# Pinning the background operations of a two-layer encoder kernel in traced order

## The chip, the cores and the metric

The kernel runs on one core of a Trainium2 chip. The metric is the device time of one execution in microseconds (us): the median of three runs of the kernel before is 1942.75 us (1942.09 to 1945.22).

## The reference

Two layers work on x of 256 rows by 2048 channels, in float32. Each layer norms its input, makes one wide projection, runs two branches on parts of it, gates and adds them, and projects once more:

```python
def hybrid_layer(x, cos, sin, norm_g, w_in, ...):
    h = rmsnorm(x, norm_g)
    proj = h @ w_in
    (c_a, c_glu, c_gate, q_down, kv_down, k_pe, m_gate, g_conv, g_mla) = jnp.split(proj, idx, axis=-1)
    y_conv = conv_branch(c_a, c_glu, c_gate, conv_w, conv_b, conv_ln_g, conv_ln_b) @ w_proj_conv
    y_mla = mla_branch(q_down, kv_down, k_pe, m_gate, cos, sin, ...) @ w_proj_mla
    y = jax.nn.sigmoid(g_conv) * y_conv + jax.nn.sigmoid(g_mla) * y_mla
    return x + y @ w_out
```

The convolution branch is a gated linear unit, a causal depthwise convolution of width 31, a layer norm over the channels, SiLU, and a SiLU gate (`c_gate`). The attention branch brings queries, keys and values up from two low-rank parts (16 heads; 128 channels without and 64 with rotary position), norms queries and keys per head, attends with a mask in chunks of 64 rows, and multiplies by a SiLU gate (`m_gate`).

## The kernel before

**Products.** Every matrix product has the activations as stationary operand and streams the weights. To keep float32 accuracy with a faster matmul format, each weight value is split into a high part and a low remainder: `split` (L178) casts a slice of the weights on ScalarE (ACT, L187) and subtracts on VectorE (DVE, L188). A slice is 128 x 1024 values (two blocks of 128 rows, up to 512 columns). For each slice TensorE (PE) issues 12 matmuls: high by high, low by high, high by low (L240 to L242), for two halves of the rows and two blocks. There are 344 slices per layer, 688 in all; `split_p` has three buffers for the high parts and three for the low ones. Weights come from HBM in pieces of two slices, through SyncE's (SP) DMA queue, into three buffers (`load`, L166).

**The order of a layer** is a list of products (`order_of_layer`, L88). Slices, counted within a layer: three blocks of the low-rank parts ("down", slices 0 to 23), two of the gated linear unit ("glu", 24 to 39), then eight times a head pair's queries and keys with values ("uq" and "ukv", two slices each) with a block of eight slices behind them: glu 2 to 7 behind the first six pairs, and the first block of the convolution's gate ("cgate" 0) behind the seventh. The eighth pair has none behind it and ends at slice 127. In before there follow mgate, gmla, pmla (32 slices each, 128 to 223), cgate 1 to 3 (224 to 247), gconv (248 to 279), pconv (280 to 311) and wout (312 to 343).

**Evacuation.** `product` (L228) traces its matmuls and then an evacuation of the two results from PSUM, which has four buffers for results (`acc`). `uq_evac` (L495) copies queries and sums their squares on ACT (L498 to L502); `ukv_evac` (L508) does so for keys and values; `glu_evac` (L682), `cgate_evac` (L838) and `mgate_evac` (L804) apply sigmoid or SiLU. `wout_evac` (L870) loads a block of the residual through SP (L873), adds it (L874), and stores it: to the output in the last layer (L876).

**Background.** After each slice `product` calls `background` (L205): one slot. It runs what is due at this slot and then, by a budget, entries of the list `fill`: 31 taps per block of the convolution (L707 on DVE, the first on ACT, L704), then the layer norm (`mean`, `centre`, `var`, `apply`: L726 to L756) and the gate's multiplication (`gated`, L845 to L859). The budget's slots are set when the first mgate product begins: 19 x 8 - 4 slots are to use up the list, and what is left is traced at the first pconv product (`drain`). For each head pair `attention` (L523) sets due slots:

```python
            def stats_soon():
                with tc.high_priority(offset=60):
                    stats()
            at_slot(STATS_AT, stats_soon)
            at_slot(QK_OUT_AT, lambda: out("qk", rows))
            at_slot(QK_BACK_AT, lambda: back_in("qk"))
```

`stats` (L527 to L553) turns the sums of squares into factors (a reciprocal root by a shift and three iterations, L293 to L298), scales the keys and rotates the queries. Then the rows are written to HBM and read back, turned in blocks of 32 (`park` L253, `fetch` L264, on GpSimd's (POOL) DMA queue); DVE transposes inside the blocks (L572), ACT and DVE split them into high and low parts (L578 to L592), PE makes the scores (L600 to L616), DVE masks them and takes maxima (L605 to L624), ACT takes exponentials with their sums (L630), DVE their reciprocal (L636). The probabilities go the same way round (L642, split by L645 and L646), and PE multiplies them by the values (L655, copied out by L659).

**What sets the order.** Each engine works through its own list in order. The kernel is traced in the order above; a scheduler then builds each engine's list by priority (traced earlier is more urgent), from its own estimate of when operands are ready. `tc.high_priority(offset=n)` makes operations as urgent as if they had been traced n instructions earlier; the slice splits have 100. `tc.keep_in_program_order` (a pin) ties one instruction behind the instruction that was traced just before it on the same engine, whatever that is. `tc.issue_after` ties a block behind a given slice's low part. In before the taps and the DMAs of `park` and `fetch` are pinned; statistics, splits, masks, norms, gates and the residual loads are not.

Of the kernel before, what the change touches and what calls it, by code (L numbers as in the profile page):

```python
# [87 lines left out]
def order_of_layer():  # L88
# [25 lines left out]
def trunk(ctx: ExitStack, tc: tile.TileContext, xT, x, g_in, pos, win, wuq, wukv, wpc, wpm, wo, cst, rows, invf, out):  # L114
    nc = tc.nc
    pool = lambda name, bufs, **kw: ctx.enter_context(tc.tile_pool(name=name, bufs=bufs, **kw))
# [136 lines left out]
    def park(src, n, home):  # L253
        d = home.tile([4, 32, 4, n // 4], F32, tag=f"t{n}", name="turn_d")
        for i in range(4):
            tc.keep_in_program_order(
                nc.gpsimd.dma_start(  # L257
                    d[:, :, i, :].rearrange("j s e -> s j e"),
                    src[32 * i : 32 * i + 32, :].rearrange("s (j e) -> s j e", j=4),
                )  # L260
            )
        return d

    def fetch(d, z):  # L264
        tc.keep_in_program_order(nc.gpsimd.dma_start(z, d.rearrange("j s i e -> (j s) (i e)")))
# [6 lines left out]
    def turn(src, n, use, dst=None):  # L272
# [14 lines left out]
    def rsqrt(y, ms):  # L287
# [5 lines left out]
        nc.vector.tensor_scalar(ti, ms.bitcast(I32), 1, None, op0=ALU.logical_shift_right)  # L293
        nc.vector.tensor_scalar(yi, ti, -1.0, RSQRT_SEED, op0=ALU.mult, op1=ALU.add)
        for _ in range(3):
            nc.vector.tensor_mul(t, y, y)
            nc.vector.scalar_tensor_tensor(t, t, -0.5, ms, op0=ALU.mult, op1=ALU.mult)
            nc.vector.scalar_tensor_tensor(y, t, 1.5, y, op0=ALU.add, op1=ALU.mult)  # L298

    def rms_factor(out_ap, sums, n):  # L300
        ms = small.tile(list(sums.shape), F32, tag=f"ms{sums.shape[-1]}", name="ms")
        nc.vector.tensor_scalar(ms, sums, 1.0 / n, EPS, op0=ALU.mult, op1=ALU.add)
# [94 lines left out]
    for l in range(DEPTH):  # L397
# [125 lines left out]
        def attention(b, pair_of=pair_of, ss_d=ss_d, kpe=kpe, ccq=ccq, ssq_t=ssq_t, gqk=gqk, nope_t=nope_t, rope_t=rope_t, rope_k=rope_k, rope_l=rope_l, o_sb=o_sb, pt_h=pt_h, pt_l=pt_l, rinv=rinv):  # L523
# [3 lines left out]
            def stats():  # L527
                ss, qk = p["ss"], p["qk"]
                nc.vector.tensor_add(ss[:, 1], ss[:, 1], ss_d[:, 2, :].unsqueeze(2).broadcast_to([P, T, 2]))
# [4 lines left out]
                nc.vector.tensor_scalar(rs, r[:, 0], float(QK**-0.5), None, op0=ALU.mult)  # L534
                st["rs"] = rs
                for t in range(T):
                    rk = r[:, 1, t, :]
                    k = qk[:, t, :, 2:4, :]
                    nc.vector.tensor_mul(k, k, rk.unsqueeze(1).unsqueeze(3).broadcast_to([P, 4, 2, 32]))
                    nc.vector.tensor_mul(  # L540
# [8 lines left out]
                nc.vector.tensor_mul(qa.rearrange("p t a h c -> p (t a) h c"), qr, both(ccq))  # L549
                nc.vector.tensor_mul(qb.rearrange("p t a h c -> p (t a) h c"), qr, both(ssq_t))  # L550
                out = qk[:, :, :, 4, :].rearrange("p t (h a) c -> p t h a c", h=2)
                nc.vector.tensor_sub(out[:, :, :, 0, :], qa[:, :, 0], qb[:, :, 1])
                nc.vector.tensor_add(out[:, :, :, 1, :], qb[:, :, 0], qa[:, :, 1])  # L553
# [14 lines left out]
            def blockwise():  # L568
                for t in range(T):
                    z = p["qk"][:, t].rearrange("p j i c -> p (j i c)")  # L570
                    with tc.issue_after(newest[0]):
                        nc.vector.transpose(z, z)  # L572

            def split_nope(which):
                z = back[:, :, 2 * which : 2 * which + 2, :].rearrange("p b h s -> p h b s")
                hi, lo = (nope_t[:, 2 * which + i].rearrange("p h (b s) -> p h b s", s=32) for i in range(2))
                if which == 0:
                    nc.scalar.activation(z, z, AF.Copy, scale=gqk)  # L578
                nc.scalar.copy(hi, z)
                nc.vector.tensor_sub(lo, z, hi.bitcast(F32))  # L580

            def split_rope(which):
                z = back[:, :, 4 + which, :]
                rt, rl = (a.rearrange("p i h (b s) -> p i h b s", s=32) for a in (rope_t, rope_l.unsqueeze(1)))
                for h in range(2):
                    own, other = halves[h], halves[1 - h]
                    nc.scalar.copy(rt[own, which, h], z[own])
                    if which == 0:
                        nc.vector.tensor_sub(rt[other, 0, h], z[own], rt[own, 0, h].bitcast(F32))
                    else:  # L590
                        nc.scalar.copy(rt[other, 1, h], z[own])
                        nc.vector.tensor_sub(rl[own, 0, h], z[own], rt[own, 1, h].bitcast(F32))  # L592

            def scores():
# [9 lines left out]
                nc.scalar.copy(sx, s0[:, :, 1, :])  # L604
                nc.vector.tensor_add(sx, s0[:, :, 0, :], sx)  # L605
# [443 lines left out]
```

## Time and profile before

| | |
|---|---|
| median of three runs | 1942.75 us (1942.09 to 1945.22) |
| profiled execution | 1944.88 us; its span from first to last instruction 1943.1 us |
| mean granted TensorE clock | 0.995 |
| PE, DVE, ACT, POOL busy | 98%, 83%, 57%, 19% of the span |
| slice splits, ACT L187 and DVE L188 | 688 each, 704.5 and 813.8 us |
| convolution taps, DVE L707 | 960, 412.7 us |
| residual loads of layer 2, SP L873 | 8 of 256 KB, 6.2 us to landing (median) |

A line of a group names source line, engine, operation, the tiles written and read with their shapes, and the count; then busy time in us, mean ns of one, the idle time of the engine just before them and what ended most of it. A line of a stretch gives, for its 40 us, the busy time and the instructions of PE, PE's weight loads, DVE, ACT and POOL, the granted clock, the share of DMA time and GB/s. A line of the timeline begins with its start and length in us; a bracket at its end names idle time before it and what ended it. Matmuls are pipelined, so their lengths overlap; their distance from start to start tells the pace.

### The profile page before, as it was taken

Reading aid. Unit: us, or ns where it says so; the run is one execution under the profiler, and the core shown is the slowest. Engines: PE = TensorE matmul, PEld = TensorE weight load, DVE = VectorE, ACT = ScalarE, POOL = GpSimd, SP = SyncE. Lnnn points to the kernel's source line nnn. Section 1 sums busy time; section 2 is a strip of 40 time slices with the busy share of each in tenths; the row PEclk is TensorE's granted clock in tenths of the full one; section 3 lists DMA queues with packets and bytes.
Section 4 is the critical chain, followed back from the end, with each engine's and each line's share of the span. In section 5 each row is a group of like instructions: output and inputs, shape, how many; then the busy total and the mean of one; then the engine's idle time right before and its main releaser. Section 6 shows DMA issues by size and latency. Waiting matters only on the chain.

```text
span 1943.1 us, 25421 instructions
## 1 busy us (share of the span) xinstructions
PE 1906.7 (98%) x8781; PEld 1601.0 (82%) x8781; DVE 1611.7 (83%) x2884; ACT 1113.0 (57%) x1782; POOL 363.1 (19%) x684
## 2 busy tenths in 40 slices
PE   9999999999999999999999999999999999999999
PEld 8888877887888887788798888878888888878887
DVE  7688898899999999565656998898999999995654
ACT  6567676766544446444555677767655444564443
POOL 0133424231000010021201324242320001001200
PEclk9999999999999999999999999999999999999999
DMA  8667766776555565576765767577765556556774
GB/s 291 220 223 251 260 215 224 264 263 225 206 195 195 206 217 208 191 245 240 270 218 201 249 221 271 204 239 252 265 222 207 194 195 211 193 214 214 241 249 141
DMA packets 85650, 437.58 MB, mean 225 GB/s; under 512 B 16896, under 2 KB 19984, under 8 KB 46608
## 3 DMA queue, kind: packets, MB, share of 16 engines
q1 hardware_dynamic: 55728, 361.44, 53.0%
q0 software_dynamic: 29792, 74.51, 11.7%
q8 instruction: 69, 1.13, 0.2%
q14 instruction: 61, 0.50, 0.1%
HBM read 395.51 MB, written 40.37 MB: 224 GB/s over the span
## 4 chain that ended last, share of the span: by engine, by line
PE 79%; DVE 8%; ACT 6%; DMA 3%; issue 2%; POOL 1%; ACTq 0%; SPq 0%; DVEq 0%; POOLq 0%
PE acc L241 26%; PE acc L242 25%; PE acc L240 25%; DVE lo L188 3%; DVE v_t L707 2%; ACT hi L187 1%; ACT pr L630 1%; PE o_ps L655 1%; PE s L616 1%; POOL turn_d L257 1%; DMA turn_d<-qk 1%; DMA pr<-turn_d 1%; ACT v_t L753 1%; DMA turned<-turn_d 1%; ACT L630 1%
## 5 line engine op out<-in xcount | busy, mean ns | idle before, releaser
L187 ACT CAST hi<-raw 128x1024 fp32r<-128x1024 f32 (+2 forms) x688 | 704.5, 1026 | 750.4 <-PE acc L242 545.4
L188 DVE TENSOR_TENSOR lo<-raw,hi 128x1024 fp32r<-128x1024 f32 (+2 forms) x688 | 813.8, 1185 | 253.0 <-ACT hi L187 250.8
L707 DVE SCALAR_TENSOR_TENSOR v_t<-u_t,cst,v_t 128x256 f32<-128x256 f32 x960 | 412.7, 476 | 1.8 <-ACT v_t L704 1.6
L241 PE MATMUL acc<-lo,h_hi 128*128 128x512 f32 (+2 forms) x864 | 334.1, 387 | 7.0 <-DVE lo L188 7.0
L241 PE MATMUL acc<-lo,hT 128*128 128x512 f32 (+2 forms) x864 | 333.7, 386 | 6.4 <-DVE lo L188 6.4
L242 PE MATMUL acc<-hi,h_lo 128*128 128x512 f32 (+2 forms) x864 | 331.6, 384 | 0.0
L242 PE MATMUL acc<-hi,hT 128*128 128x512 f32 (+2 forms) x864 | 331.5, 384 | 0.0
L240 PE MATMUL acc<-hi,h_hi 128*128 128x512 f32 (+2 forms) x864 | 299.1, 384 | 3.1 <-ACT hi L187 2.7
L240 PE MATMUL acc<-hi,hT 128*128 128x512 f32 (+2 forms) x864 | 298.7, 384 | 0.4 <-ACT gate L809 0.4
L257 POOL DMA_DIRECT2D turn_d<-gate x176 | 95.6, 551 | 582.8 <-ACT gate L842 402.6
L241 PEld LDWEIGHTS acc<-lo,h_hi 128*128 128x128 f32 x864 | 163.2, 189 | 41.2 <-DVE lo L188 11.9
L241 PEld LDWEIGHTS acc<-lo,hT 128*128 128x128 f32 x864 | 162.8, 188 | 39.9 <-DVE lo L188 10.4
L240 PEld LDWEIGHTS acc<-hi,h_hi 128*128 128x128 f32 x864 | 162.0, 189 | 34.9 <-ACT hi L187 4.3
L240 PEld LDWEIGHTS acc<-hi,hT 128*128 128x128 f32 x864 | 162.1, 189 | 31.6 <-ACT hi L187 1.0
L242 PEld LDWEIGHTS acc<-hi,h_lo 128*128 128x128 f32 x864 | 163.3, 189 | 29.5
L242 PEld LDWEIGHTS acc<-hi,hT 128*128 128x128 f32 x864 | 162.9, 189 | 29.7
L257 POOL DMA_DIRECT2D turn_d<-su x128 | 69.7, 551 | 286.7 <-DVE su L687 257.0
L241 PE MATMUL acc<-lo,yT 128*128 128x512 f32 x256 | 100.0, 391 | 1.4 <-DVE lo L188 1.4
L242 PE MATMUL acc<-hi,yT 128*128 128x512 f32 x256 | 99.7, 389 | 0.0
L241 PE MATMUL acc<-lo,oT 128*128 128x512 f32 x256 | 99.6, 389 | 0.0
L241 PE MATMUL acc<-lo,ycT 128*128 128x512 f32 x256 | 99.6, 389 | 0.0
L242 PE MATMUL acc<-hi,oT 128*128 128x512 f32 x256 | 99.6, 389 | 0.0
(203 smaller groups left out, 2606.3 us busy)
## 6 DMA issues: line engine op xcount, KB each, us to landing
raw<-in_win SPq DMA_DIRECT2D x192, 1024.0 KB, 4.9
raw<-in_wpm SPq DMA_DIRECT2D x32, 1024.0 KB, 4.8
raw<-in_wpc SPq DMA_DIRECT2D x32, 1024.0 KB, 4.8
raw<-in_wo SPq DMA_DIRECT2D x32, 1024.0 KB, 5.7
raw<-in_wukv SPq DMA_DIRECT2D x16, 1024.0 KB, 6.3
turned<-turn_d POOLq DMA_DIRECT2D x50, 256.0 KB, 4.9
raw<-in_wuq SPq DMA_DIRECT2D x16, 768.0 KB, 4.5
turn_d<-qk POOLq DMA_DIRECT2D x128, 96.0 KB, 3.7
```

The costliest lines, as they stand in the source:

```text
L187: nc.scalar.copy(hi, r)
L188: ins = nc.vector.tensor_sub(lo, r, hi.bitcast(F32))
L240: nc.tensor.matmul(pts[t][:, :n], sh, hi[:, kk, :], start=first, stop=False)
L241: nc.tensor.matmul(pts[t][:, :n], sh, lo[:, kk, :], start=False, stop=False)
L242: nc.tensor.matmul(pts[t][:, :n], sl, hi[:, kk, :], start=False, stop=last)
L257: nc.gpsimd.dma_start(d[:, :, i, :].rearrange("j s e -> s j e"), src[32 * i : 32 * i + 32, :].rearrange("s (j e) -> s j e", j=4),)
L616: nc.tensor.matmul(s1[:, h, :], qa, ka, start=n == 0, stop=n == len(terms) - 1)
L630: nc.scalar.activation(pr[:, :, h, t : t + nkeys // P, :].rearrange("p j x c -> p x j c"), s[:, h, :].rearrange("p (x j c) -> p x j c", j= ...
L655: nc.tensor.matmul(o_ps[:, h, kt * P :], v[j][:, kt, h, :], pt[i][:, h, queries], start=n == 0, stop=n == len(todo) - 1,)
L707: nc.vector.scalar_tensor_tensor(dst, src, w, dst, op0=ALU.mult, op1=ALU.add)
L753: nc.scalar.activation(v[:, j, :], v[:, j, :], AF.Silu, bias=C[:, C_LB + ct : C_LB + ct + 1], scale=C[:, C_LG + ct : C_LG + ct + 1],)
```

## The change

Three wrappers make every call on them a pinned one: `vec` for DVE, `act` for ACT, `dma` for POOL. All operations of the background go through them: the transposes and uses of turned blocks, the reciprocal roots, the statistics, the splits, masks, maxima and exponentials, the taps, norms and gates. The splits of slices and most evacuations do not. The statistics get a priority offset of 200 instead of 60. The residual loads are pinned on SP. The convolution gate's blocks 1 to 3 stand directly behind the last pair (slices 128 to 151), so that mgate is 152 to 183, gmla 184 to 215 and pmla 216 to 247; the slots of the budget are now set when cgate 1 begins, again at slice 128, with the same number. The weights' columns are laid out in the new order on the host.

```diff
     for kind, s in (
-        ("mgate", "win"), ("gmla", "win"), ("pmla", "wpm"),
-        ("cgate", "win"), ("gconv", "win"), ("pconv", "wpc"), ("wout", "wo"),
+        ("cgate", "win"), ("mgate", "win"), ("gmla", "win"), ("pmla", "wpm"),
+        ("gconv", "win"), ("pconv", "wpc"), ("wout", "wo"),
     ):
...
+    class InOrder:
+        def __init__(self, engine):
+            self.engine = engine
+        def __getattr__(self, name):
+            return lambda *a, **k: tc.keep_in_program_order(getattr(self.engine, name)(*a, **k))
+    vec, act, dma = InOrder(nc.vector), InOrder(nc.scalar), InOrder(nc.gpsimd)
...
-            nc.vector.transpose(z if dst is None else dst.rearrange("p c (i s) -> p i c s", i=4), z)
+            vec.transpose(z if dst is None else dst.rearrange("p c (i s) -> p i c s", i=4), z)
...
-                nc.vector.tensor_add(ss[:, 1], ss[:, 1], ss_d[:, 2, :].unsqueeze(2).broadcast_to([P, T, 2]))
+                vec.tensor_add(ss[:, 1], ss[:, 1], ss_d[:, 2, :].unsqueeze(2).broadcast_to([P, T, 2]))
...
-                nc.scalar.copy(hi, z)
-                nc.vector.tensor_sub(lo, z, hi.bitcast(F32))
+                act.copy(hi, z)
+                vec.tensor_sub(lo, z, hi.bitcast(F32))
...
             def stats_soon():
-                with tc.high_priority(offset=60):
+                with tc.high_priority(offset=200):
                     stats()
...
-                nc.vector.tensor_mul(v, v, wide(rstd))
+                vec.tensor_mul(v, v, wide(rstd))
...
-            nc.vector.transpose(z, z)
+            vec.transpose(z, z)
...
-            nc.sync.dma_start(xt, (x if l == 0 else x1_dram)[t, :, blk])
+            tc.keep_in_program_order(nc.sync.dma_start(xt, (x if l == 0 else x1_dram)[t, :, blk]))
...
             elif kind == "mgate":
-                if i == 0:
-                    budget["slots"] = 19 * 8 - 4
...
             elif kind == "cgate":
+                if i == 1:
+                    budget["slots"] = 19 * 8 - 4
```

More of the change, by code (lines that the diff above doesn't have):

```diff
@@ L586, in split_rope @@
                     own, other = halves[h], halves[1 - h]
-                    nc.scalar.copy(rt[own, which, h], z[own])
+                    act.copy(rt[own, which, h], z[own])
                     if which == 0:
-                        nc.vector.tensor_sub(rt[other, 0, h], z[own], rt[own, 0, h].bitcast(F32))
+                        vec.tensor_sub(rt[other, 0, h], z[own], rt[own, 0, h].bitcast(F32))
                     else:
-                        nc.scalar.copy(rt[other, 1, h], z[own])
-                        nc.vector.tensor_sub(rl[own, 0, h], z[own], rt[own, 1, h].bitcast(F32))
+                        act.copy(rt[other, 1, h], z[own])
+                        vec.tensor_sub(rl[own, 0, h], z[own], rt[own, 1, h].bitcast(F32))
             def scores():
@@ L635, in scores @@
                         )
-                nc.vector.reciprocal(rinv[:, :, 2 * b : 2 * b + 2], sums)
+                vec.reciprocal(rinv[:, :, 2 * b : 2 * b + 2], sums)
                 st["pr"] = pr.rearrange("p j h x c -> p (j h x c)")
@@ L658, in values @@
                         )
-                nc.scalar.copy(o_sb[:, 2 * b : 2 * b + 2, :], o_ps)
+                act.copy(o_sb[:, 2 * b : 2 * b + 2, :], o_ps)
                 pairs.pop(b)
             def stats_soon():
-                with tc.high_priority(offset=60):
+                with tc.high_priority(offset=200):
                     stats()
```

100 lines of the change are left out of this document (48 added, 52 removed).

## The prediction

> **What bounds the kernel now.** I read the shares by engine first, then TensorE's own waits, then the time stretch by stretch, then two stalls instruction by instruction.
>
> ```profile
> PE 1906.7 (98%) x8781; PEld 1601.0 (82%) x8781; DVE 1611.7 (83%) x2884; ACT 1113.0 (57%) x1782; POOL 363.1 (19%) x684
> ```
>
> TensorE (PE) is busy 98%, so at most some 36 us of it is idle. Nothing here can win more than a few per cent, and everything that can be lost is a wait of PE. Its waits, longest first in total:
>
> ```profile
> engine line waited for: us in total, times, longest us
> PE acc L241 <- DVE lo L188: 14.8, 21, 1.8
> PE o_ps L655 <- ACT pv L645: 6.9, 6, 1.3
> PE acc L240 <- ACT hi L187: 4.4, 3, 2.7
> ```
>
> PE waits for the low halves of the weight slices (DVE, L188) and for the attention's splits, not for DMAs. To count also the matmuls that ran slowly, I took PE's timeline: undisturbed 128x512 matmuls start 0.227 us apart (a slice of 12 takes 2.72 us). Every excess over the usual distance, summed, is 55.7 us: 4.9 at the start; 16.3 and 17.2 in the pair stages (160 to 520 us, and 1120 to 1480 us in layer 2); 7.4 per layer around 760 and 1720 us, where the convolution is normed and gated; 1.9 around 957 us; the rest is small.
>
> ```profile
> 320.00:360.00 40.00, 37.17 (x171) 30.72 (x172) 36.48 (x79) 29.75 (x71) 12.97 (x25) 0.96 0.65 202
> 760.00:800.00 40.00, 36.08 (x147) 27.93 (x146) 32.03 (x49) 29.26 (x42) 1.60 (x3) 0.96 0.51 180
> 800.00:840.00 40.00, 40.00 (x178) 33.11 (x177) 21.10 (x22) 16.01 (x16) 5.47 (x10) 1.00 0.64 228
> ```
>
> An undisturbed 40 us holds 178 matmuls (third row); the gating stage has 147, at a granted clock of 0.96. One stall there, and what follows it:
>
> ```profile
> 780.39 0.68 PE L240 MATMUL acc<-hi,h_hi 128*128 128x512 f32 x2
> 782.87 0.50 PE L241 MATMUL acc<-lo,h_hi 128*128 128x512 f32 x1 [1.81 <-DVE lo L188]
> ...
> 784.16 0.63 PE L242 MATMUL acc<-hi,h_lo 128*128 128x512 f32 x1
> 784.59 0.63 PE L241 MATMUL acc<-lo,h_hi 128*128 128x512 f32 x1
> ```
>
> After about 2 us without work the matmuls start 0.43 us apart for some ten matmuls: a long stall costs about 2.0 us on top.
>
> **The rule of the stalls.** There are three buffers of slices, so the high half of slice k is cast when PE begins slice k-2 (0.2 us after it, in nearly every slice). An operation that stands on ACT or DVE behind slice k-1 cannot run earlier than PE's slice k-3. So I number places by the slices issued before them: when PE needs at slice p what ACT does at place p+3, the margin is 0 and PE must wait. And between two low halves DVE must not have more work than PE has slices left. In before, two boundaries of products have margin 0: slices 92 and 116, where the evacuation of a query product (L498 to L502) stands at places 95 and 119. They lose 2.9 us (with slice 95) and 4.2 us (with slice 120) of the pair stage's 16.3. What DVE does behind slice 118 there:
>
> ```profile
> 323.11 1.22 DVE L188 TENSOR_TENSOR lo<-raw,hi 128x1024 fp32r<-128x1024 f32 x1
> 324.25 0.95 DVE L646 TENSOR_TENSOR pv<-pr,pv 128x768 fp32r<-128x768 f32 x1
> ...
> 330.80 0.15 DVE L624 TENSOR_TENSOR nb<-nb,rs_p 128x4 f32<-128x4 f32 x1
> 332.27 1.22 DVE L188 TENSOR_TENSOR lo<-raw,hi 128x1024 fp32r<-128x1024 f32 x1 [1.32 <-ACT hi L187]
> ```
>
> The 19 operations from 324.25 to 330.95 take 6.7 us; their groups' busy time per instruction sums to 7.7, so a block costs 0.87 of such a sum.
>
> **The change, part by part.** The order in which the two built programs list each engine's instructions tells more than the diff. A pin ties an operation behind the instruction traced just before it on its engine; the slice splits stay free. The amount of work is the same (2,884 DVE instructions); only places move.
>
> *Statistics sooner, everything in traced order (DVE, ACT).* In before the statistics (L529 to L553) are spread thinly over ten slices (part of them floats up to 16 places ahead). In after they stand in one block, mixed with the masks, maxima, probability splits and convolution taps of the pair before, between two low halves:
> - place 95: 40 operations, 11 taps x 0.430 + 10 small ones of the reciprocal root x 0.18 + L642 0.97 + L646 0.95 + L580 0.68 + L623 0.65 + the rest = 14.2, x 0.87 = 12.4 us (before 7.8 x 0.87 = 6.8);
> - place 119: 14.1 x 0.87 = 12.3 (before 6.7, and 3.1 behind the next slice); place 131: 13.3 x 0.87 = 11.6 (before 2.5, with 5.2 at 126); place 107: 8.4 x 0.87 = 7.3.
>
> And the evacuations of query products now have margin 0 at four boundaries: 92, 104, 116, 128 (places 95, 107, 119, 131).
>
> The price at slice 116, from PE's arrival there (319.38 us): in before the low half of 118 ended 4.95 us later; three small operations more make it 5.3. Then 12.3 and the next low half 1.18: 18.8. PE has meanwhile three slices (8.2), 16 score and 12 value matmuls (3.1 by their usual distances), and may go 0.3 into slice 119: 11.6. Loss 7.2 us, and 2.0 for the slow clock. At 92 ACT first does the six rope casts, the gain and the first nope cast (3.6 us), then the cast of slice 94; its low half ends about 4.4 us after PE's arrival: 4.4 + 12.4 + 1.2 - 11.6 = 6.4. At 128 likewise, 5.0 + 11.6 + 1.2 - 11.6 = 6.2. At 104 the evacuation ends some 5.1 us after PE's arrival, against 2.2 us of scores and values: 2.9, with a short tail 3.5. What remains: about 0.8 at 78, 0.4 at 158. Sum per layer: 7.2 + 2.0 + 6.4 + 6.2 + 3.5 + 1.2 = 26.5, against 16.3 and 17.2 now: +9.7 per layer, **+19.4**. The floor is what the blocks cost if each begins at the earliest place, behind a low half that ends 2.4 us after PE's arrival: 4.4 + 4.3 + 3.6 + 1.6 + 1.2 = 15.1, which is 1.2 to 2.1 us per layer less than now. The other end, slow clock after every one of the four: +6 per layer.
>
> The trace grants 0.96 after a stall of 2 us. [...]
>
> *Convolution gate's blocks behind the last pair.* Slices 128 to 151 are now cgate 1 to 3, then mgate, gmla, pmla: the same matmuls. It hides a late evacuation at slice 168 (0.7 us in before; in after its place leaves margin 6); this is in the 26.5. The tap budget starts at slice 128 as before, so the taps end in the same stretch.
>
> *Norming and gating.* Here pinning should cut the burst, and does not: eight L750 multiplications (4.9 x 0.87 = 4.3 us) now stand together at place 278, ACT has the table load and 4, then 8 Silu at places 279 and 280. The burst is the same, seven slices later, and now the first products of pconv (slice 280) need its results (L858, L859 at place 281). Following DVE from place 276 on, PE waits about 1.0, 0.4, 2.2 and 1.0 us, and once for the clock: 5.5 instead of 7.4, **-4** over both layers. Bounds: -4 to +2 per layer, by the sums of that block on ACT.
>
> *Residual loads pinned (L873, SP).* In layer 1 each is issued one weight piece later and still lands some us before its use. At the layer's end the two transposes are now apart, so the wait of 1.56 us at 957 us goes: **-1.6**. In layer 2 a pinned load stands behind the store traced before it. Now the eight loads were out by 1884 us:
>
> ```profile
> L873 SPq DMA_DIRECT2D xres<-x_dram x8: 319/328/538, 1851.3 to 1883.9; - x8
> 1939.00 0.69 DVE L874 TENSOR_TENSOR xres<-acc,xres 128x512 f32<-128x512 f32 x1 [0.44 <-PE acc L242]
> ```
>
> After it, the last load waits for the store of the row block beside it, which waits for the addition at 1937.87. So load (0.4 to issue, landing 3.4 to 8.2 by these loads, 4.1 the median of the last stores, which I take as the queues are empty), and only then the last addition: **+4.1**, from 3.4 to 8. No engine has work left to hide it.
>
> **Sum.** +19.4 - 4 - 1.6 + 4.1 = +17.9, say 18. The profiled execution took 1944.88 us (span 1943.1), 2.1 over the median of 1942.75; 18 on the median is **1961**.
>
> **Rivals.**
> - *The blocks hide in waits that exist.* DVE waits 35.7 us in total for the exponentials (L636); work pinned ahead of it could fill that. Then each boundary pays the floor: -3.3 - 4 - 1.6 + 4.1 = -5, that is 1938, and up to 1946 as one or two fall short. For it: the block sizes are certain, their starts are not. Against: in before the low half ahead of the block ends 4.5 to 5 us after PE's arrival, not 2.4. Within 0.2% (3.9 us, about what a measurement tells from no change): 10%.
> - *Faster: the gate stage runs without a stall.* If the pinned splits of slices 274 to 283 all precede the burst, 14.8 us go; with the floor at the boundaries 1942.75 - 14.8 - 3.3 - 1.6 + 4.1 = 1927. It decides when DVE has under 1.5 us between two low halves there; the built order has 4.3. 7%.
> - *Slower still: the rows come back late.* A pair's rows go out when its block ends (eight DMAs x 0.55 on POOL, 3.7 to land, 1.1 and 5.8 back: 15 us), and the transposes (L572) follow seven slices later, about 16 to 19 us. If DVE waits 2 us there at four boundaries, and the clock falls at each, +14 per layer: about 1978. 13%.
> - *The pins bind nothing*, because a free split stands between: then 1943. The moved places speak against it; under 1%, in the 10%.
>
> The forecast has 70%. Chances: faster 0.07, same 0.10, slower 0.83. The range leaves out the floor's half and the top: 1945 to 1979.
>
> **What would show it.** Right: stalls of 3 to 5 us at slices 92, 116 and 128, blocks of 12 us on DVE between two L188; PE's loss in the pair stages near 26 us per layer; a pause of about 4 us before the last L874; L636 without its wait. Wrong: the pair stages lose 16 us or less, or the gating stage reaches 178 matmuls per 40 us.

## The result, and the profile after

The changed kernel takes 1953.32 us (median of 4 runs, 1953.05 to 1953.72) against 1943.72 us for the kernel before (4 runs on the same chip): a ratio of 1.005, 95% interval 1.0032 to 1.0067. That is 9.6 us slower. In the profiled executions the span grows from 1943.1 to 1952.0 us. The forecast was 1961 us: the direction holds, the forecast rise of 18 us is about double the measured one.

The shares by engine are nearly those of before, so they do not tell where 9 us went:

```profile
PE 1910.5 (98%) x8781; PEld 1607.7 (82%) x8781; DVE 1614.0 (83%) x2884; ACT 1111.4 (57%) x1778; POOL 363.0 (19%) x684
```

TensorE's (PE's) waits do. In the changed kernel every call through a wrapper is recorded with the wrapper's line, L124; the tile names tell which operation it is. The slices' low halves are now L199, their matmuls L251 to L253, the scores L609 to L625, the values L664, the residual load and addition L880 and L881.

```profile
PE s L625 <- ACT qk_t L124: 9.8, 6, 2.2
PE acc L252 <- DVE lo L199: 6.3, 7, 1.8
PE acc L251 <- ACT hi L198: 3.8, 3, 2.8
```

Waits for low halves fell from 14.8 to 6.3 us; waits of the scores (`s`) for ACT's casts of queries and keys (`qk_t`) rose from 2.4 to 9.8 us, and those for DVE's low parts of them from 1.0 to 6.2. By stretches of 40 us (busy time of PE, its weight loads, DVE, ACT, POOL; granted clock; DMA share; GB/s):

```profile
360.00:400.00 40.00, 36.04 (x157) 29.86 (x156) 33.06 (x72) 27.96 (x61) 12.52 (x23) 0.91 0.66 228
760.00:800.00 40.00, 39.41 (x172) 31.68 (x170) 36.27 (x59) 24.81 (x35) 4.29 (x8) 1.00 0.60 216
800.00:840.00 40.00, 38.08 (x166) 30.73 (x166) 28.27 (x35) 22.46 (x27) 5.46 (x10) 1.00 0.65 230
```

The gating stage got better: 172 matmuls at full clock in the stretch that had 147 at 0.96, and the rest of its stalls moved into the next one (166 instead of 178). The stretch at 360 us got worse: its clock is 0.91, where before it was 1.00. Counted as the prediction counted (every excess of the distance between two matmuls over the usual one, by the slice at which it falls), in us, layer 1 / layer 2:

| where | before | forecast | after |
|---|---|---|---|
| slice 92 | 2.3 / 3.8 | 6.4 | 7.2 / 6.2 |
| slices 101 to 104 | 1.6 / 1.6 | 3.5 | 1.6 / 1.6 |
| slices 116 to 120 | 5.0 / 5.1 | 9.2 | 5.9 / 5.9 |
| slices 126 to 131 | 2.4 / 2.4 | 6.2 | 7.8 / 6.9 |
| pair stage, slices 60 to 168, in all | 16.2 / 17.1 | 26.5 | 23.4 / 21.8 |
| norming and gating, slices 250 to 299 | 7.4 / 7.3 | 5.5 | 4.3 / 4.3 |
| end of the layer, slices 300 to 343 | 1.8 / 0.2 | 0.2 | 0.9 / 0.2 |
| last matmul to the end of the span | 4.1 | 8.2 | 7.2 |

Summed over both layers: pair stages +11.9, gating -6.1, end of layer 1 -0.9, tail +3.1, start of the kernel +1.0 (6.2 after 5.2; it lay between 5.2 and 6.8 in the other runs): +9.0, against a span longer by 8.9. Within the pair stages slices 92 and 126 to 131 lose 17.2 us more over both layers and slices 116 to 120 lose 1.7 more, while the small waits at the other slices lose 7.0 less.

**Slice 128.** The worst stall of the change, on PE's timeline:

```profile
365.87 0.35 PE L625 MATMUL s<-qk_t 128*128 128x256 f32 x1 [1.02 <-DVE qk_t L124]
366.67 0.38 PE L609 MATMUL s<-qk_t 128*128 128x256 f32 x1 [0.45 <-DVE qk_t L124]
369.19 0.80 PE L625 MATMUL s<-qk_t 128*128 128x256 f32 x2 [2.13 <-ACT qk_t L124]
...
370.97 0.48 PE L610 MATMUL s<-qk_t 128*128 128x128 f32 x1 [0.36 <-DVE qk_t L124]
```

PE arrives at the scores at 364.7 us and waits 4.0 us in four pieces. From the first score at 365.87 to the first matmul of slice 128 at 375.81 it takes 9.9 us, of which 2.9 are waits; the 28 matmuls for scores and values take 7.0 us instead of the usual 3.1. The granted clock is 0.50 from 368.94 to 375.76 (the lines are in the last section), and PE works in 6.2 us of that: at half speed that is an estimated 3.1 of the 7.8 us lost here. The rest is the waits and the gaps around single matmuls. What it waits for, on ACT's timeline:

```profile
363.87 2.54 ACT L124 CAST qk_t<-qk 64x256 fp32r<-64x256 f32 x6 [0.65 <-DVE qk L124]
366.44 0.72 ACT L124 ACTIVATE qk<-qk,gqk 128x512 f32<-128x512 f32 x1
...
367.57 1.04 ACT L198 CAST hi<-raw 128x1024 fp32r<-128x1024 f32 x1
368.52 0.61 ACT L124 CAST qk_t<-qk 128x512 fp32r<-128x512 f32 x1
```

The casts of the returned rows begin 0.8 us before PE arrives, and end 4.4 us after. In the kernel before the scores of this pair began behind slice 125, two slices ahead of slice 128, and their casts 5.5 us ahead of the first score (348.2 against 353.7), not 2.0. Slice 92 is alike: waits of 3.5 us, then a granted clock of 0.50 from 249.48 to 256.30.

**Slice 116.** Here the block on DVE ends the stall, as forecast, but it adds little: 4.0 us are lost ahead of the slice's first matmul, in waits for casts and in slow clock, as in the kernel before (granted clock 0.50 from 322.80 to 326.21 us there), and 1.9 us at slice 119 behind the block. DVE and then PE:

```profile
327.80 1.22 DVE L199 TENSOR_TENSOR lo<-raw,hi 128x1024 fp32r<-128x1024 f32 x1
328.93 0.95 DVE L124 TENSOR_TENSOR pv<-pr,pv 128x768 fp32r<-128x768 f32 x1
...
340.47 2.35 DVE L199 TENSOR_TENSOR lo<-raw,hi 128x1024 fp32r<-128x1024 f32 x2
```

```profile
329.05 0.63 PE L251 MATMUL acc<-hi,h_hi 128*128 128x512 f32 x1
329.47 0.63 PE L252 MATMUL acc<-lo,h_hi 128*128 128x512 f32 x1
...
341.74 0.50 PE L252 MATMUL acc<-lo,h_hi 128*128 128x512 f32 x1 [1.63 <-DVE lo L199]
```

41 operations stand between the two low halves and take 11.4 us. PE, which arrived at 324.05, is late for its first slice (329.05), runs slowly for five matmuls (0.43 us apart; the granted clock is 0.50 from 327.98 to 331.39), and still catches up with DVE at 341.74, where it waits 1.63 us.

**The end.** SP (the first line merges two stores, the second of which is issued when its sum is ready) and then DVE:

```profile
1930.16 14.54 SPq L883 DMA_DIRECT2D out<-xres  x2
1944.75 0.42 SPq L880 DMA_DIRECT2D xres<-x_dram  x1
```

```profile
1943.64 0.69 DVE L881 TENSOR_TENSOR xres<-acc,xres 128x512 f32<-128x512 f32 x1 [4.71 <-PE acc L253]
1947.86 0.69 DVE L881 TENSOR_TENSOR xres<-acc,xres 128x512 f32<-128x512 f32 x1 [3.53 <-DMA xres<-x_dram]
```

The last load is issued at 1944.75, behind the store of the block beside it, and the last addition waits 3.53 us for it.

### The profile page after: what moved, and what is told of

Its sections match the earlier page's. It is cut to its first block, busy times and chain, and to the rows that moved or that the text cites. A ratio compares the mean times of both kernels' runs of the same rounds, so it can differ in the third digit from the quotient of the medians.

```text
span 1952.0 us, 25418 instructions
## 1 busy us (share of the span) xinstructions
PE 1910.5 (98%) x8781; PEld 1607.7 (82%) x8781; DVE 1614.0 (83%) x2884; ACT 1111.4 (57%) x1778; POOL 363.0 (19%) x684
## 4 chain that ended last, share of the span: by engine, by line
PE 85%; DVE 6%; DMA 4%; ACT 2%; issue 2%; POOL 1%; SPq 0%; DVEq 0%; ACTq 0%; POOLq 0%
PE acc L252 27%; PE acc L251 27%; PE acc L253 27%; DVE v_t L124 2%; DVE lo L199 1%; DMA turn_d<-qk 1%; PE o_ps L664 1%; ACT hi L198 1%; DMA qk<-turn_d 1%; POOL turn_d L124 1%; PE s L625 1%; DMA turned<-turn_d 1%; DVE qk_t L124 1%; ACT qk_t L124 1%; DVE turned L124 0%
## 5 line engine op out<-in xcount | busy, mean ns | idle before, releaser
L199 DVE TENSOR_TENSOR lo<-raw,hi 128x1024 fp32r<-128x1024 f32 (+2 forms) x688 | 815.0, 1185 | 267.5 <-ACT hi L198 265.4
L124 DVE SCALAR_TENSOR_TENSOR v_t<-u_t,cst,v_t 128x256 f32<-128x256 f32 x960 | 411.8, 476 | 2.8 <-ACT v_t L124 2.5
L253 PE MATMUL acc<-hi,h_lo 128*128 128x512 f32 (+2 forms) x864 | 331.7, 384 | 0.0
L253 PE MATMUL acc<-hi,hT 128*128 128x512 f32 (+2 forms) x864 | 330.1, 383 | 0.0
L251 PE MATMUL acc<-hi,h_hi 128*128 128x512 f32 (+2 forms) x864 | 299.9, 385 | 3.5 <-ACT hi L198 2.8
L251 PE MATMUL acc<-hi,hT 128*128 128x512 f32 (+2 forms) x864 | 298.2, 383 | 0.6 <-ACT junk L511 0.6
L251 PEld LDWEIGHTS acc<-hi,h_hi 128*128 128x128 f32 x864 | 163.2, 190 | 34.1 <-ACT hi L198 3.5
L253 PEld LDWEIGHTS acc<-hi,h_lo 128*128 128x128 f32 x864 | 163.5, 189 | 29.6
L251 PEld LDWEIGHTS acc<-hi,hT 128*128 128x128 f32 x864 | 161.9, 188 | 30.5 <-ACT junk L511 0.8
L253 PEld LDWEIGHTS acc<-hi,hT 128*128 128x128 f32 x864 | 162.3, 188 | 29.5
L124 POOL DMA_DIRECT2D turn_d<-gate x176 | 95.8, 551 | 168.2 <-DVE gate L874 105.9
L124 POOL DMA_DIRECT2D turn_d<-qk x128 | 69.7, 552 | 272.1 <-DVE qk L124 226.1
L124 POOL DMA_DIRECT2D turn_d<-su x128 | 69.8, 552 | 268.5 <-DVE su L696 199.7
L124 POOL DMA_DIRECT2D turned<-turn_d x82 | 44.7, 547 | 388.9 <-DVE ln_stats L124 271.7
L253 PE MATMUL acc<-hi,ycT 128*128 128x512 f32 x256 | 99.5, 390 | 0.9 <-DVE ycT L124 0.9
```

The lines of the kernel that those rows point to most:

```text
L124: return lambda *a, **k: tc.keep_in_program_order(getattr(self.engine, name)(*a, **k))
L199: ins = nc.vector.tensor_sub(lo, r, hi.bitcast(F32))
L251: nc.tensor.matmul(pts[t][:, :n], sh, hi[:, kk, :], start=first, stop=False)
L253: nc.tensor.matmul(pts[t][:, :n], sl, hi[:, kk, :], start=False, stop=last)
```

## The experiments

First the order in which the built programs list their instructions. With the priority offset of the statistics set back from 200 to 60 and all else as changed, the lists of all five engines are the same as the changed kernel's. "Statistics sooner" does nothing beside the pins, so it was not run by itself.

All runs are shown against the kernel before on the same chip. Losses of PE are us per layer by slice, layer 1 / layer 2.

| kernel | median us | ratio, 95% interval | slices 60-159 | 160-249 | 250-299 | last matmul to end |
|---|---|---|---|---|---|---|
| before (its profile) | 1943.72 | | 15.5 / 16.4 | 0.7 / 0.7 | 7.4 / 7.3 | 4.1 |
| changed | 1953.32 | 1.0050 (1.0032-1.0067) | 23.4 / 21.8 | 0 / 0 | 4.3 / 4.3 | 7.2 |
| changed, loads free | 1950.43 | 1.0035 (1.0023-1.0047) | 23.6 / 22.5 | 0 / 0 | 4.3 / 4.3 | 4.2 |
| before, statistics pinned | 1982.99 | 1.0200 (1.0186-1.0214) | 24.3 / 33.0 | 10.5 / 9.4 | 4.9 / 5.0 | 4.1 |
| changed, pairs free | 1938.27 | 0.9977 (0.9967-0.9987) | 15.8 / 15.8 | 0 / 0 | 3.8 / 3.8 | 7.2 |
| before, gate moved | 1941.52 | 0.9994 (0.9985-1.0003) | 15.2 / 14.6 | 0 / 0 | 11.1 / 4.3 | 4.2 |
| before, gating pinned | 1933.96 | 0.9953 (0.9939-0.9966) | 16.4 / 14.8 | 0.7 / 0.7 | 2.5 / 2.5 | 4.2 |
| changed, short taps | 1939.86 (one run) | | 18.3 / 16.4 | 0.8 / 0.8 | 2.2 / 2.2 | 7.2 |
| changed, pairs and loads free | 1937.04 | 0.9960 (0.9947-0.9972) | 16.9 / 16.8 | 0 / 0 | 3.7 / 3.8 | 4.2 |
| the same, scores one slot earlier | 1926.71 | 0.9910 (0.9895-0.9924) | 11.3 / 12.1 | 0 / 0 | 3.7 / 3.8 | 4.1 |
| changed, casts traced earlier | 1972.73 | 1.0152 (1.0138-1.0166) | 36.9 / 29.0 | 0 / 0 | 4.3 / 4.3 | 7.2 |
| changed, scores one slot earlier | 1981.92 | 1.0199 (1.0185-1.0213) | 29.4 / 29.0 | 0.7 / 0 | 4.6 / 17.4 | 7.4 |
| changed, statistics free | 1931.85 | 0.9940 (0.9927-0.9952) | 12.0 / 13.5 | 0 / 0 | 3.1 / 3.0 | 7.2 |
| before, gating pinned, scores one slot earlier | 1932.66 | 0.9946 (0.9933-0.9960) | 13.0 / 12.7 | 4.0 / 2.4 | 2.9 / 3.0 | 4.2 |

**The loads free.**

```diff
-            tc.keep_in_program_order(nc.sync.dma_start(xt, (x if l == 0 else x1_dram)[t, :, blk]))
+            nc.sync.dma_start(xt, (x if l == 0 else x1_dram)[t, :, blk])
```

> The changed kernel with the residual loads free again (no pin on SP), all else as changed. Theory: after the last matmul the changed kernel needs 7.2 us where the one before needed 4.1, because its last load stands behind a store; without the pin the end is 4.1 us again and the time 3.1 us less, 1950.2. The wait of 1.6 us at the end of layer 1 may come back: then 1951. Rival: the longer end comes from the later evacuations, not from the pin; then 1953.3 as changed, and the pause before the last addition stays.

Measured 1950.43 us; the end is 4.2 us again, and the last addition waits for PE, not for its load:

```profile
1945.29 0.69 DVE L881 TENSOR_TENSOR xres<-acc,xres 128x512 f32<-128x512 f32 x1 [0.44 <-PE acc L253]
```

The pin costs 3 us at the end, as forecast. The end of layer 1 does not wait here (0.2 us), though the loads are free.

**The statistics pinned, nothing else.**

```diff
-            nc.vector.scalar_tensor_tensor(y, t, 1.5, y, op0=ALU.add, op1=ALU.mult)
+            vec.scalar_tensor_tensor(y, t, 1.5, y, op0=ALU.add, op1=ALU.mult)
...
-                nc.vector.tensor_add(ss[:, 1], ss[:, 1], ss_d[:, 2, :].unsqueeze(2).broadcast_to([P, T, 2]))
+                vec.tensor_add(ss[:, 1], ss[:, 1], ss_d[:, 2, :].unsqueeze(2).broadcast_to([P, T, 2]))
...
```

> The kernel before, with one part of the change alone: the statistics of the pairs (L529 to L553 with their reciprocal root) pinned in traced order on DVE; everything else free, the convolution gate's blocks in their old place, loads free. In the built order this alone already puts 40, 29, 41 and 40 operations on DVE between two low halves at places 95, 107, 119 and 131, as in the changed kernel. Theory: these blocks are the loss; TensorE loses 23.5 and 21.9 us in the pair stages as in the changed kernel (16.3 and 17.2 before), and the time is 1943.7 + 11.9 = 1955.6, 1952 to 1958, with the gating stage as before. Rival: the loss comes from the pins on the splits, the scores' operations and the maxima; then the pair stages stay within 2 us of before and the time is 1942 to 1946.

Measured 1982.99: the place was right, the size missed. In layer 1's pair stage PE loses 24.3 us, with the blocks of the changed kernel, so these pins alone make a loss of that size. Layer 2 loses 33.0 us, 11 more than in the changed kernel, and both layers lose some 10 us at slices 160 to 249, which the change does not. There the first block after the last pair is mgate in the old order, and the built order piles up 30 operations at place 171, 22 of them taps, among them mgate's evacuation; DVE reaches the next low half 14 us later. DVE and then PE:

```profile
494.21 1.22 DVE L198 TENSOR_TENSOR lo<-raw,hi 128x1024 fp32r<-128x1024 f32 x1
495.34 5.63 DVE L717 SCALAR_TENSOR_TENSOR v_t<-u_t,cst,v_t 128x256 f32<-128x256 f32 x14
500.89 0.69 DVE L822 TENSOR_TENSOR gate<-gate,rinv 128x512 f32<-128x512 f32 x1
```

```profile
510.65 0.79 PE L251 MATMUL acc<-lo,h_hi 128*128 128x512 f32 x1 [1.25 <-DVE lo L198]
```

A pin on one group moves others too: the taps wait behind the statistics of the last pair, and the evacuation behind the taps.

**The pairs free, the rest as changed.**

```diff
-                vec.tensor_add(ss[:, 1], ss[:, 1], ss_d[:, 2, :].unsqueeze(2).broadcast_to([P, T, 2]))
+                nc.vector.tensor_add(ss[:, 1], ss[:, 1], ss_d[:, 2, :].unsqueeze(2).broadcast_to([P, T, 2]))
...
-                act.copy(hi, z)
-                vec.tensor_sub(lo, z, hi.bitcast(F32))
+                nc.scalar.copy(hi, z)
+                nc.vector.tensor_sub(lo, z, hi.bitcast(F32))
...
```

> The changed kernel with all operations of the attention pairs free again (statistics, transposes, splits, masks, maxima, exponentials); taps, norming, gating, turns, the gate's new place and the pinned loads stay. The built order of the pair stage is then that of the kernel before. Theory: the pair stages lose 16 to 17 us again instead of 23.5 and 21.9, the gain of 6 us in the gating stage stays, as its pins stay: 1953.3 - 11.9 = 1941.4, 1939 to 1944. Rival: the gating stage won only because the pair stage's blocks shifted the taps; then its 6 us are lost with them and the time is about 1947.

Measured 1938.27, some 15 us below the changed kernel and 3 us below the forecast of this run. The pair stages lose 15.8 us again and the gating stage 3.8. The pins on the pairs cost 12 to 15 us; without them the rest of the change is a gain.

**The gate's blocks moved, nothing else.** The edit is the change's first and last hunk.

> The kernel before with the convolution gate's blocks behind the last pair, nothing else. Theory: the move gains only the late evacuation at slice 168, 0.7 us per layer: 1942.3, 1941 to 1944, and the gating stage still loses 6 to 7 us per layer. Rival: the move, not the pins, is what shortens the gating stage, since the rows are parked earlier: then 1938.

Measured 1941.52, with an interval that takes in no change. The loss at slice 168 is gone; the gating stage went to both sides of its 7.4 and 7.3 us, 11.1 in layer 1 and 4.3 in layer 2. Layer 1:

```profile
760.00:800.00 40.00, 32.71 (x130) 24.63 (x129) 32.87 (x53) 32.14 (x43) 1.60 (x3) 0.91 0.43 155
```

So the move alone does not shorten the gating stage; unpinned, its order can fall either way.

**The norming and gating pinned, nothing else.**

```diff
-                nc.vector.tensor_mul(v, v, wide(rstd))
+                vec.tensor_mul(v, v, wide(rstd))
...
-            nc.vector.transpose(z, z)
+            vec.transpose(z, z)
...
```

> The kernel before, with the norming and gating of the convolution alone pinned in traced order on DVE and ACT; the gate's blocks stay in their old place, pairs and loads stay free. Theory: it is these pins that shorten the gating stage; TensorE loses 4 us per layer there instead of 7.4, and the time is 1943.1 - 6.8 = 1936.3, 1934 to 1939. Rival: the gain needs the gate's blocks moved, which lets the built order change (the move alone gave 11.1 us in layer 1 and 4.3 in layer 2): then 7 us per layer stay and the time is 1943, within 2.

Measured 1933.96, 2.3 us below the forecast of this run: PE loses 2.5 us per layer instead of 7.4 and 7.3. Its stretch at 760 us keeps the full clock:

```profile
760.00:800.00 40.00, 39.32 (x168) 30.80 (x167) 34.93 (x52) 31.22 (x45) 1.61 (x3) 1.00 0.58 204
```

These pins are the good part of the change: this kernel is 9.6 us faster than the one before. Both expectations were too high for the gating stage, and the rival did not hold: the gain does not need the move of the gate.

**Short taps.**

```diff
-                        vec.scalar_tensor_tensor(dst, src, w, dst, op0=ALU.mult, op1=ALU.add)
+                        vec.scalar_tensor_tensor(dst[:, :32], src[:, :32], w, dst[:, :32], op0=ALU.mult, op1=ALU.add)
```

> The changed kernel with the convolution's taps computed on 32 of 256 columns (the rest of each tap is left out). In layer 1 the block at place 119 has the same operations in nearly the same order; the 11 taps in a block take about 0.35 us less each, so a block is some 3.9 us shorter. Theory: at slices 92 and 128 TensorE waits for the scores' casts on ACT, not for the block, and these losses stay (7.2 and 7.8 us, each within 1.5), as does the 4.0 at 116, while the 1.9 behind 119 goes: the pair stage of layer 1 loses 20 to 22 us instead of 23.4. Rival, the step of the prediction: the block sets these losses, and each falls by 3.9 us or to its floor: about 12 us. The time of the whole is not judged, since DVE has 0.3 ms less work.

In layer 1 slice 92 loses 4.1 us (7.2), 104 1.3 (1.6), 116 4.0 and nothing behind it (4.0 and 1.9), 128 5.6 (7.8): 18.3 in all. Neither theory gave this. The 1.9 behind slice 119 went and the 4.0 at 116 stayed, as the theory had it; but 92 and 128 fell by 3.1 and 2.2. At 128 PE still waits in the scores:

```profile
365.58 0.50 PE L625 MATMUL s<-qk_t 128*128 128x256 f32 x2 [1.02 <-ACT qk_t L124]
```

The wait is shorter because the casts begin earlier, 1.6 us before PE's arrival instead of 0.8: a shorter block at slice 116 ends the next pair's statistics earlier (at PE's slice 118 instead of 119), and its rows go out earlier. So a block costs twice: a wait for the low half behind it, and a delay of the next pair's rows. In layer 2 the built order differs: no block stands at place 119 and slice 116 loses nothing, while a block of 41 operations and 11.2 us stands at place 107 and slice 104 loses some 6 us; 92 and 128 lose some 2.7 each.

**Pairs and loads free.** Both edits above together.

> The changed kernel with the attention pairs' operations free and the residual loads free: the gate's new place and the pins on taps, norming, gating and turns stay. Theory: the parts add up, 1938.3 - 3.1 = 1935.2, 1933 to 1937, below the kernel before. Rival: without the pinned loads the end of layer 1 waits again (1.7 us before) and the end gains less: 1937 to 1939.

Measured 1937.04, at the edge of the two expectations: 1.2 us below the version with pinned loads. The trace shows the end shorter by 3.0 us (4.2 against 7.2) and the end of layer 1 unchanged, but 2.1 us more in the pair stages (slices 92 and 344 + 92: 3.8 and 3.7 instead of 2.3), and 1.1 more ahead of slice 60. Such differences of a boundary also lie between the layers of one run (2.3 and 3.8 in before).

**The same with the scores one slot earlier.**

```diff
-STATS_AT, QK_OUT_AT, QK_BACK_AT, ROPE_AT, NOPE_AT, SCORES_AT = 1, 4, 8, 13, 14, 17
-P_OUT_AT, P_BACK_AT, P_AT, VALUES_AT = 20, 24, 28, 30
+STATS_AT, QK_OUT_AT, QK_BACK_AT, ROPE_AT, NOPE_AT, SCORES_AT = 1, 4, 8, 13, 14, 16
+P_OUT_AT, P_BACK_AT, P_AT, VALUES_AT = 19, 23, 27, 29
```

> The version with pairs and loads free, and the scores and all that follows them in a pair (rows of probabilities out and back, their split, values) one slot earlier. The built order then has no block over 14 operations on DVE in the last pairs (19 and 15 before). Theory: a boundary loses because the scores' operations meet the evacuation of a query product; one slot apart, the pair stage loses 10 to 13 us per layer instead of 15.8: 1925 to 1931. Rival: the casts of the scores are now later than TensorE at each pair, and it waits there: 1937 or more.

Measured 1926.71, 10.3 us less than without the shift, as the theory had it. No block on DVE of over 6.3 us is left in the pair stages, and no wait of the scores for casts is over 0.7 us:

```profile
PE acc L252 <- DVE lo L199: 10.1, 14, 1.0
...
PE s L625 <- ACT qk_t L588: 1.5, 2, 0.7
```

It is the fastest version of this study, 17 us (0.9%) below the kernel before.

**Casts traced one slot earlier, all pins kept.**

```diff
-STATS_AT, QK_OUT_AT, QK_BACK_AT, ROPE_AT, NOPE_AT, SCORES_AT = 1, 4, 8, 13, 14, 17
+STATS_AT, QK_OUT_AT, QK_BACK_AT, ROPE_AT, NOPE_AT, SCORES_AT = 1, 4, 8, 12, 13, 17
```

> The changed kernel with the transposes of a pair's returned rows and the casts behind them (rope and nope parts) traced one slot earlier; blocks of 38, 32, 31 and 42 operations on DVE stay at places 95, 107, 119 and 131. Theory: at slices 92 and 128 TensorE waits in the scores for these casts, because they begin only 0.8 us before its arrival; one slot (2.7 us) earlier, the waits for them fall from 9.8 us in the whole run to under 4, and the pair stage loses 18 to 20 us per layer instead of 23.4 and 21.8: about 1946. Rival, the prediction's step: the blocks set the loss, which stays: 1953. Second rival: the rows are not back earlier (at slice 128 the last one landed 0.3 us after DVE asked for it), so that DVE waits for them and nothing is won: 1952 to 1956, with a wait of DVE for rows of some 2 us at slice 128.

Measured 1972.73: all three were wrong, the theory most. Traced earlier did not mean done earlier. At layer 1's slice 128 the first row's transpose waits for its DMA, and the second stands behind the next low half, whose high half waits for PE, which waits for an evacuation on ACT (3.13 us at slice 126). DVE, then PE:

```profile
369.36 0.98 DVE L124 STREAM_TRANSPOSE qk<-qk 128x768 f32<-128x768 f32 x1 [1.72 <-DMA qk<-turn_d]
376.78 1.23 DVE L199 TENSOR_TENSOR lo<-raw,hi 128x1024 fp32r<-128x1024 f32 x1 [6.43 <-ACT hi L198]
377.92 0.97 DVE L124 STREAM_TRANSPOSE qk<-qk 128x768 f32<-128x768 f32 x1
```

```profile
382.13 0.55 PE L625 MATMUL s<-qk_t 128*128 128x256 f32 x1 [5.08 <-DVE qk_t L124]
```

With everything pinned, DVE idles 6.43 us there while the transposes stand behind the low half. The wait of DVE for rows that the second rival named is there, and is not what costs most.

**Scores one slot earlier, all pins kept.** The edit is that of the fastest version, on the changed kernel.

> The changed kernel, all pins kept, with the scores and what follows them one slot earlier, as in the version that took 1926.7 us with the pairs free. Blocks of 37, 37 and 37 operations stay at places 95, 107 and 131, 20 at 119. Theory: without the pins the shift won 10 us by parting the scores from the evacuation; with the pins the casts still come when they did, and the scores now ask for them 2.7 us sooner, so at least 20 us per layer are lost in the pair stages and the time is 1950 or more. Rival: only the meeting of scores and evacuation matters, not the pins: 12 us per layer, 1934.

Measured 1981.92. The pair stages lose 29.4 and 29.0 us, within the theory's "at least 20 us"; what it had not is a wait of 14.22 us at the first pconv product of layer 2, whose operands are late by the gating on ACT. The edit that wins 10.3 us with free pairs loses 29 us with pinned ones.

**The statistics free, all else as changed.** The reverse of the edit of the run with the statistics pinned.

> The changed kernel with the statistics alone free (with their reciprocal root); the pairs' transposes, splits, scores and probabilities stay pinned. The built order has 26, 15 and 29 operations at places 95, 119 and 131 and no block over 12 at 107. Theory: most of the loss in the pair stages comes from the pinned statistics; 17 to 19 us per layer are lost there instead of 23.4 and 21.8, the gating stage loses 2.5 as with its pins alone, and the time is 1953.3 - 9 - 3.5 = 1941, 1938 to 1944. Rival: the pinned splits and scores are as bad by themselves: 1950.

Measured 1931.85, 9 us below the forecast of this run: the pair stages lose 12.0 and 13.5 us, less than in the kernel before. What remains there is slice 92 (6.7 and 7.1), where a block of 26 operations is left; slice 128 loses 1.9 and 2.2. So, with the statistics free, the pins on transposes, splits, scores and probabilities are no loss; together with the run that pins the statistics alone, this shows that the pins on the statistics make the loss.

**Before, with the gating pinned and the scores earlier.** The edits of two runs above together, on the kernel before.

> The kernel before with two edits: the norming and gating pinned (which alone gave 1934.0) and the scores with what follows them one slot earlier (which gave 10.3 us with the pairs and loads free). Theory: the parts stand in different stages and add up: 1934.0 - 10.3 = 1923.7, 1921 to 1926. Rival: the shift crowds the taps into the gating stage and its gain is lost: 1927 to 1930.

Measured 1932.66: the parts do not add up, and not for the rival's reason either. The pair stages and the gating stage do win (12.7 to 13.0, and 3), but slices 153 to 160 now lose 6.4 and 4.8 us, among them 4.0 and 2.4 at the first evacuations of mgate (L819). With the gate's blocks behind the last pair, as in the fastest version, there is no such evacuation beside the last pair's attention. The comparison suggests that the move pays where attention reaches past the last pair; it does not show it, since the two kernels also differ in other pins, among them those on the turned rows' transposes and on the first taps on ACT. Alone the move showed 1.6 us, within what can be told from none.

## Why the prediction was right in direction and too large

**The blocks: right.** They were forecast at 12.4, 7.3, 12.3 and 11.6 us at places 95, 107, 119 and 131; DVE spent 12.9, 6.8, 11.4 and 12.8 us there in layer 1 (waits included). That the pinned statistics make them is shown by both runs on the statistics. But the step from block to loss, that PE waits for the low half behind the block, accounts for little of the rise: 1.7 of the 18.9 us by which slices 92, 116 to 120 and 126 to 131 rose over both layers. The cause of the rise was right, the way it reaches PE mostly was not.

**Slice 116, 9.2 us forecast, 5.9 measured: this term was mis-sized.** The cover was right: from PE's arrival to the resumption 17.7 us pass, less 11.6 us of own work gives 6.1. Two things were too large. The low half ahead of the block ended 4.9 us after the arrival instead of 5.3, and the block took 11.4 instead of 12.3: some 1.2 us. And the 2.0 us for the slow clock were counted on top, while the slow matmuls ran inside the time in which PE would have waited for DVE anyway. A loss of speed ahead of a wait is part of the wait. The forecast's 9.2 also stands against 5.0 in the kernel before: the change adds 0.9 here.

**Slice 104, 3.5 forecast, 1.6 measured: mis-sized.** ACT ended the freeing of the first buffer 3.6 us after PE's arrival (291.3 against 287.75), not 5.1: the squares of the second result came after it and were wrongly counted into PE's wait.

**Slices 92 and 128, 6.4 and 6.2 forecast, 7.2 / 6.2 and 7.8 / 6.9 measured: right size by luck, wrong step.** The forecast took PE's wait from the low half behind the block. There was no such wait. PE waited before that, 3.5 and 4.0 us in the scores, for the casts of the returned rows, and paid in slow clock, in layer 1 an estimated 3.1 us at each; after that the block lay in its shadow. The rival "the rows come back late" named this neighbourhood, but had DVE waiting for DMAs: DVE waited 0.3 us at slice 128. That rival took 15 us for the rows' way; they needed 19.9, from the statistics' last operation (342.9) to the second transpose (362.8). The run with short taps shows that the block does set part of it, by way of the rows.

**Pair stages in sum:** +11.9 instead of +19.4; 116 and 104 make up 10.4 of what was too much over both layers, 92 and 128 give 2.9 back.

**Gating, -4 forecast, -6.1 measured.** The waits came where forecast (1.0, 0.4, 2.2 and 1.0 us forecast; 0.8, 0.3, 1.8 and 0.9 at slices 278, 279, 280 and 282), but without the slow clock: the granted clock is 1.00 from 768 to 816 us. The reason given, that pinning does not cut the burst, was too dim: the gating's pins alone, in the old place, leave 2.5 us.

**End of layer 1, -1.6 forecast, -0.9 measured, by the wrong cause.** The wait is gone also with the loads free, and in the kernel before it is gone with only the gate's blocks moved or only the statistics pinned, and shrinks with only the gating pinned (1.1). So the pin on the loads is not needed for it; what ends it stays open.

**Tail, +4.1 forecast, +3.1 measured**, by the cause that was named: the run with free loads has 4.2 us again. The load landed in 3.1 us after its issue (1944.75 to 1947.86), less than the 3.4 to 8.2 of the rows before. The DMA share is 0.00 from 1940 to 1944, so nothing was in the load's way.

**The rivals.** The blocks did not hide, though DVE's waits for the exponentials fell from 35.7 to 16.4 us, so that about half of these waits was filled. The gating stage was not without a stall, and the pins did bind. The rival of the late rows had its sum wrong: +14 us per layer on top of the forecast would be 1989 us, in place of its pair stages 1970, not 1978. The sum was 9.0 us too large (17.9 against the 8.9 of the span): 7.5 in the pair stages, 2.1 in the gating and 1.0 in the tail, less 0.7 at the end of layer 1 and 1.0 at the start.

## What to carry to other kernels

Here it paid to pin a chain whose consumers follow at once (the norming and gating, -9.6 us), and to leave free what a round trip through DRAM stands behind (the statistics, whose pins made the loss: 1953.3 us with them, 1931.9 without): a pin makes an operation wait for whatever was traced before it. Judge an order by what stands between two operations that feed the bottleneck, and by what goes out behind that block. Do not add a price for a slow clock to a wait that comes after it (2.0 us too much at slice 116); add it only where nothing later makes the engine wait anyway.

## What the runs showed of the hardware that was not expected

In the traces of this case TensorE's clock changes in whole steps of time. In all 14 the granted clock is 1.00 or 0.50, and a slow phase inside the kernel lasts 3.41, 6.83, 10.24 or 13.65 us. Within a trace all slow phases begin on one grid of 3.41 us. Matmuls of 128x512 start 0.23 us apart at full clock and 0.43 in a slow phase. The stretches around the slow phase at slice 128 of the changed kernel:

```profile
365.53:368.94 3.41, 0.74 (x2) 0.37 (x2) 3.31 (x9) 3.34 (x7) 0.00 (x0) 1.00 0.78 274
368.94:375.76 6.82, 6.22 (x26) 5.79 (x27) 6.21 (x24) 3.96 (x17) 0.00 (x0) 0.50 0.06 24
375.77:379.18 3.41, 3.41 (x17) 2.84 (x16) 2.86 (x10) 3.40 (x10) 1.04 (x2) 1.00 0.02 5
```

Here the fall goes with how busy PE was in the step before, not with the length of a single wait, of which none at slice 128 is over 2.13 us. At slices 92 and 128 of the changed kernel's layer 1 PE was busy for 0.74 of the 3.41 us before the fall, and each slow phase lasts 6.83 us. Cut along that grid, from 20 us after the start to 3 us before the last matmul's end, the 14 traces have 44 steps at full clock in which PE was busy for less than half of the time; the clock fell behind 43 of them. Of the 7682 in which it was busy for 57% or more, it fell behind one. Between these shares it went both ways.

By the distances of the matmuls, 0.43 against 0.23 us, a slow phase costs an estimated half of the time that PE works in it; its length alone does not tell the price. In the run with the scores one slot earlier and all pins kept, PE waits 14.22 us:

```profile
1782.92:1786.33 3.41, 0.00 (x0) 0.00 (x0) 3.41 (x7) 3.39 (x7) 0.94 (x2) 1.00 0.00 0
1786.33:1796.57 10.24, 0.00 (x0) 0.00 (x0) 4.86 (x11) 10.16 (x14) 0.13 (x1) 0.50 0.48 154
1796.57:1799.98 3.41, 3.20 (x8) 2.54 (x9) 3.22 (x7) 2.76 (x6) 0.00 (x0) 0.50 0.00 0
```

The clock is slow for 13.65 us, but PE works in only 3.20 of them, an estimated loss of 1.6 us. At slices 92 and 128 of the changed kernel's layer 1 it works in 6.2 of 6.8 us, an estimated 3.1 us each. So a sum for this kernel should carry the price of a stall as a range, an estimate from these steps: from nothing to half of one step (1.7 us) or of two (3.4 us), and more where PE works through a longer phase.
